# Steps of the weights' sums: every fourth tile of queries instead of every third, and two for each head of the linear attention

## The chip, the cores and the metric

The kernel runs on one core of one Trainium2 chip. The time is the device time of one execution in microseconds (us), and the profile is of one execution of the same program. PE is the engine of the matrix products, ACT the one of the activations, DVE the vector engine, POOL the GpSimd engine, SP the engine that mostly issues transfers. ACTq stands for transfers that ACT's instruction stream issues.

## The reference

One step of a layer of a hybrid decoder over 1024 new tokens of a prompt and 8 x 8 tokens of running sequences. The token mixing has two branches, softmax attention with a forget gate (8 heads) and gated linear attention (4 heads), then a GeGLU network with a convolution:

```
hn = rmsnorm(x, g_pre_mix)
q_a, k_a, v_a, logf, q_b, k_b, v_b, log_alpha, r_b, gate_a, gate_b = project_mixer_inputs(hn, ...)
o_a = attn_fn(q_a, k_a, v_a, logf)                  # forgetting attention
o_b, gla_state = gla_fn(q_b, k_b, v_b, log_alpha)   # linear attention, in chunks
o_b = rmsnorm(o_b, g_gla) * silu(r_b)
merged = sigmoid(gate_a) * (o_a @ w_proj_a) + sigmoid(gate_b) * (o_b @ w_proj_b)
x = x + rmsnorm(merged @ w_out, g_post_mix)
u = rmsnorm(x, g_pre_ffn) @ w_up                    # then convolution, gelu(g) * a, @ w_down
y = x + rmsnorm(f, g_post_ffn)
```

## The kernel before, in words

All products are made of three single products of split operands (high times high, high times low, low times high). The products with `w_up` use a scheme of Strassen's kind, which needs sums and differences of blocks of `w_up`. These sums are built early and in DRAM, by transfers alone: `ws_step` makes one step of it. Step number n issues four plain copies of quarter blocks of `w_up` into `d_ws[n]` from ACT's stream (line 195, 512 rows of 512 bytes, 256 KB each), and up to four adding transfers from POOL's stream (line 200) which belong to blocks n-1, n-2 and n-3: two that add from `w_up`, two that add one `d_ws` into another. Blocks 2 to 21 exist, so the steps run from 2 to 24, with one empty step behind them; the last steps have no copies any more. The sums are read in the network's stage, from about 1300 us on. `ws_step` gets a `pace`, an ACT instruction and a POOL instruction: its copies stand behind the first and its adding transfers behind the second.

The stages in order of time: normalisation and the first products (0 to 104 us), the forgetting attention of the prompt (104 to 459, four pairs of heads j, n = 0 to 15 tiles of queries in each), the attention of the running sequences (459 to 640), the linear attention, one head after another (640 to about 1050), merging and the output product, then the network (1300 on).

In the forgetting attention, each tile's `scores` run one tile ahead of `turn` and `values`; softmax exponentials are ACT's (line 745), 128 elements wide for a head's first tile and 128 more for each next one, eight tiles to a head. Columns of the input projection (`mm`) that are needed later are cut into units of six products and spread between the tiles by `slot()`. In the linear attention each head has a part of levels, then a part of eight chunks: for every chunk c the output `o` (line 122, three products of `ath`, `vh` and three of the running state `sth`, `qe`), copied out by ACT (`ob`, line 1251) since there is one buffer for `o`; the state's product `S`, added into `st` by DVE; and its high part `sth` made by ACT. Between them stand the decay of the next head (`e`, lines 860 to 862), the gate of the output (lines 1229 to 1231, on rows loaded from `d_r` by SP at line 1221), and units of the next head's projections with their evacuations (`q`, `k`, line 630); the groups `mm` of these units take three buffers in turn, so that a fourth group waits for the evacuation of the first. The head ends with a norm on DVE (line 1304) and turns on PE. Here `pace` is the exponential of line 1187 and the subtraction on POOL of line 1214, which stand just ahead of the first chunk. POOL then has the `km` of line 1292, needed at the end of the chunks, and the clearing of `ath` for the next head (line 1104).

The framework's scheduler sets the order of each engine's instructions from the order in which they are written and their dependences. Its hardware transfers, SP's and ACT's together, take eight completion counters in turn, so that a transfer waits until the one eight before it is done.

## Time and profile before

| | us |
|---|---|
| median of 3 runs (lowest, highest) | 2026.95 (2025.34, 2031.42) |
| the profiled execution's own time | 2028.32 |
| its span in the trace | 2026.6 |
| PE busy | 1953.4 (96%) |
| DVE, ACT, POOL busy | 1315.1, 910.8, 461.5 |

The span is the time from the first to the last recorded instruction; the execution's own time is 1.7 us longer. A row of the trace with `x2` merges equal instructions that follow each other, and its second number is then the time from the first one's start to the last one's end. What stands in brackets at a row's end is the idle time of the engine before it and what ended it.

### The profile page before, as it was taken

To read this page: it belongs to the slowest core of one execution; us is meant where nothing else is said; L and a number is where in the kernel's file an instruction comes from. 1 tells how busy PE (TensorE), PEld (TensorE's weight loads), DVE (VectorE), ACT (ScalarE), POOL (GpSimd) and SP (SyncE) were. 2 spreads that over 40 slices of the span, in tenths; PEclk is the share of its full clock that TensorE was granted. 3 is DMA by queue.
4 is the path that set the end of the run, shared out by engine and by line. 5 is a ranking of instruction groups with operands and counts; after the bars stand their busy time and mean duration, and the time that the engine had idled before them with its cause. 6 is when DMAs were issued, how large, how long until landed. Compare 5 with 4: busy or idle time off the path is not lost.

```text
span 2026.6 us, 35542 instructions
## 1 busy us (share of the span) xinstructions
PE 1953.4 (96%) x13681; PEld 1789.9 (88%) x13681; DVE 1315.1 (65%) x2635; ACT 910.8 (45%) x1734; POOL 461.5 (23%) x610
## 2 busy tenths in 40 slices
PE   6999999999999899999999999999999999999998
PEld 5899999997888788888989977899999999977886
DVE  6566665663334786868464457877677677758686
ACT  5344544442333465564544333454444444545552
POOL 2032323232110432313012221123223334210000
PEclk9999999999999999999999999999999999999999
DMA  4387979797883152423387442143444555657575
GB/s 139 96 200 182 230 184 204 172 223 269 284 267 110 43 136 60 120 60 99 105 263 233 151 156 104 41 143 129 145 132 144 195 181 171 224 194 244 175 251 158
DMA packets 302431, 335.25 MB, mean 165 GB/s; under 512 B 23327, under 2 KB 234575, under 8 KB 298165
## 3 DMA queue, kind: packets, MB, share of 16 engines
q1 hardware_dynamic: 216501, 217.37, 34.9%
q0 software_dynamic: 39488, 79.15, 15.4%
q10 hardware_dynamic: 46272, 36.44, 5.7%
q8 instruction: 108, 1.77, 0.4%
q14 instruction: 62, 0.51, 0.1%
HBM read 265.78 MB, written 113.30 MB: 187 GB/s over the span
## 4 chain that ended last, share of the span: by engine, by line
PE 77%; DVE 9%; DMA 6%; ACT 4%; issue 2%; POOL 1%; ACTq 1%; DVEq 0%; SPq 0%; POOLq 0%
PE mm L122 37%; PE dn L122 15%; PE u L122 9%; PE tp L125 5%; PE o L122 4%; PE S L122 3%; PE y L122 3%; DVE wv L128 2%; DMA d_ob<-oo 2%; DVE wlo L128 1%; DMA smk<-in_consts 1%; ACTq L195 1%; PE sm L122 1%; DMA m<-d_ob 1%; DVE act L128 1%
## 5 line engine op out<-in xcount | busy, mean ns | idle before, releaser
L122 PE MATMUL mm<-act,whi 128*128 128x384 f32 (+2 forms) x3568 | 891.1, 331 | 5.5 <-DVE act L128 3.9
L122 PEld LDWEIGHTS mm<-act,whi 128*128 128x128 f32 (+1 forms) x3568 | 617.1, 189 | 15.6 <-DVE act L128 5.4
L122 PE MATMUL mm<-act,wlo 128*128 128x384 f32 (+2 forms) x1784 | 583.2, 327 | 0.0
L122 PEld LDWEIGHTS mm<-act,wlo 128*128 128x128 f32 (+1 forms) x1784 | 336.3, 189 | 0.5
L128 DVE TENSOR_TENSOR wlo<-wraw,whi 128x1024 fp32r<-128x1024 f32 (+1 forms) x111 | 135.1, 1217 | 57.3 <-ACT whi L134 53.9
L134 ACT ACTIVATE whi<-wraw 128x1024 fp32r<-128x1024 f32 (+1 forms) x113 | 115.9, 1025 | 87.2 <-PE mm L122 79.1
L131 DVE SCALAR_TENSOR_TENSOR cv<-u,cw,cv 128x1104 f32<-128x1104 f32 x84 | 112.8, 1363 | 13.0 <-ACT cv L1556 13.0
L122 PE MATMUL dn<-dh,hhi 128*128 128x512 f32 x264 | 105.0, 400 | 2.4 <-ACT hhi L134 2.4
L122 PE MATMUL dn<-dh,hlo 128*128 128x512 f32 x264 | 104.8, 397 | 0.3 <-DVE hlo L128 0.3
L122 PE MATMUL dn<-dl,hhi 128*128 128x512 f32 x264 | 105.0, 398 | 0.0
L122 PE MATMUL y<-wo,act 128*128 128x512 f32 x416 | 99.8, 397 | 1.3 <-DVE wo L128 1.1
L122 PEld LDWEIGHTS y<-wo,act 128*128 128x128 f32 x416 | 77.1, 188 | 21.2 <-DVE wo L128 2.2
L134 ACT ACTIVATE sh<-sr 128x512 fp32r<-128x512 f32 x80 | 50.3, 633 | 87.1 <-PE u L122 33.3
L722 POOL TENSOR_SCALAR_AFFINE_SELECT bd<-cb 128x128 f32<-128x128 f32 x64 | 36.8, 582 | 179.8 <-DVE mx L739 163.3
L745 ACT ACTIVATE s<-s,ng 128x128 f32<-128x128 f32 (+3 forms) x64 | 49.6, 775 | 48.8 <-DVE ng L743 46.5
L420 ACT ACTIVATE spl<-mm 128x384 f32<-128x384 f32 (+1 forms) x72 | 33.6, 468 | 84.4 <-PE mm L122 74.4
L128 POOL TENSOR_TENSOR wv<-wv,k 128x512 f32<-128x512 f32 (+1 forms) x28 | 51.8, 1868 | 73.2 <-ACT wv L1128 72.1
L122 PE MATMUL mm<-bh,whi 128*128 128x384 f32 (+1 forms) x192 | 63.0, 328 | 3.2 <-ACT bh L134 2.6
L134 ACT ACTIVATE pth<-tp 128x512 fp32r<-128x512 f32 (+2 forms) x96 | 43.5, 488 | 49.3 <-PE tp L125 16.9
L735 DVE CUSTOM_DVE_ANT_0 s<-S,cb 128x512 f32<-128x512 f32 (+2 forms) x80 | 40.7, 527 | 37.9 <-PE S L122 32.4
L1556 ACT ACTIVATE cv<-u,cw 128x1104 f32<-128x1104 f32 x42 | 54.9, 1308 | 22.0 <-issue 10.8
L200 POOL DMA_DIRECT2D d_ws<-in_w_up x40 | 53.9, 1542 | 41.1 <-DMA d_ws<-in_w_up 40.7
(470 smaller groups left out, 4281.5 us busy)
## 6 DMA issues: line engine op xcount, KB each, us to landing
wraw<-in_w_in SPq DMA_DIRECT2D x52, 512.0 KB
wraw<-in_w_up SPq DMA_DIRECT2D x44, 512.0 KB
d_ws<-in_w_up ACTq DMA_DIRECT2D x80, 256.0 KB
sr<-d_ws SPq DMA_DIRECT2D x80, 256.0 KB
draw<-in_w_down SPq DMA_DIRECT2D x77, 256.0 KB
d_h<-cv POOLq DMA_DIRECT2D x44, 256.0 KB, 5.0
d_s<-spl POOLq DMA_DIRECT2D x44, 256.0 KB, 4.8
d_ws<-in_w_up POOLq DMA_DIRECT2D x40, 256.0 KB, 9.2
```

Of the source, the lines that this page charges most:

```text
L122: return record(pe.matmul(out, **kw))
L125: return record(pe.transpose(*args))
L128: eng.tensor_tensor(out=out, in0=a, in1=b, op=op)
L131: return dve.scalar_tensor_tensor(out=out, in0=a, scalar=s, in1=b, op0=op0, op1=op1)
L134: act.activation(out, src, AF.Copy)
L195: act.dma_start(out=d, in_=y)
L200: pool.dma_start(out=d_ws[i][d], in_=src, max_dma_last_dim=4 * P * 4, accum_op=ALU.add)
L420: act.activation(t[:, o:o + n], ps[:, :n], AF.Copy)
L722: pace[1] = pool.affine_select(out=bd, in_=cb[:, qc], pattern=[[-1, P]], compare_op=ALU.is_ge, fill=NEG, base=0, channel_multiplier=1)
L735: dve.tensor_tensor_reduce(out=s[:, k0:k0 + m], in0=ps[:, :m], in1=cb[:, k0:k0 + m], scale=1.0, scalar=-3.0e38, op0=ALU.add, op1=ALU.max, ...
L745: pace[0] = act.activation(s[:, :nk], s[:, :nk], AF.Exp, bias=ng, accum_out=sm)
L1556: act.activation(c, u[:, 2:], AF.Identity, scale=cw[:, 2, m:m + 1], bias=cw[:, 3, m:m + 1])
```

## The change

In the forgetting attention a step is made at n = 1, 5, 9, 13 of each pair of heads, and no more at n = 1, 4, 7, 10, 13: 16 steps in place of 20. In the linear attention each head makes two steps in place of one, with the same pace: 8 in place of 4. The number of all steps, 24, and their transfers stay the same.

```
@@ hybrid_step, forgetting attention
             if n < 15:
                 heads[2 * j + (n + 1) // 8][0]((qt + 1) % 8)
-                if n % 3 == 1:
+                if n % 4 == 1:
                     ws_step(*pace)
                 slot()
@@ hybrid_step, linear attention
             pace[1] = pool.tensor_tensor(out=ql, in0=qe[:, :T], in1=f(qh), op=ALU.subtract)
             ws_step(*pace)
+            ws_step(*pace)
             sil = []
```

Before, the steps of the forgetting attention were numbers 2 to 21 and held all 80 copies; the four heads of the linear attention had numbers 22 to 25, with 4, 2, 1 and 0 adding transfers. Now the forgetting attention has numbers 2 to 17, and the heads have 18 and 19, 20 and 21, 22 and 23, 24 and 25: 8, 8, 0 and 0 copies on ACT, and 8, 8, 6 and 1 adding transfers on POOL. Lines behind 1215 have a number higher by one in the changed kernel.

ACT, in the first head's chunks, before: from the copy of the first chunk's output on. `ob` is that copy, `wv` and `k` are casts of operands, `q` is the evacuation of the next head's first group of products, `e` its decay, `sth` the state's high part.

```order
L1251 ACTIVATE ob_8165<-o_8167 128x256
L1264 ACTIVATE jk_8182,gss_8166<-ob_8165 128x256
L134 ACTIVATE wv_8084<-vT_8077 128x1024
L134 ACTIVATE wv_8075<-tp_8087 128x512
L134 ACTIVATE wv_8075<-tp_8094 128x512
L630 ACTIVATE q_8157<-mm_8158 128x384
L134 ACTIVATE k_1478_7542<-tp_8101 32x128 x2
L860 ACTIVATE e_1536_8123<-tp_8121,ba_5499 128x384
L134 ACTIVATE k_1479_7543<-tp_8101 32x128 x2
L861 ACTIVATE e_1536_8123<-e_1536_8123 128x384
L134 ACTIVATE sth_8178<-st_8176 128x256
```

ACT at the same place now. Two copies (`d_ws_18_86` and `d_ws_18_87`) stand a few rows higher, ahead of the casts `wv`.

```order
L195 DMA d_ws_18_88_149<-in_w_up 512x1x128
L134 ACTIVATE k_1478_7510<-tp_8069 32x128 x2
L195 DMA d_ws_18_89_150<-in_w_up 512x1x128
L134 ACTIVATE k_1479_7511<-tp_8069 32x128 x2
L195 DMA d_ws_19_90_151<-in_w_up 512x1x128
L195 DMA d_ws_19_91_152<-in_w_up 512x1x128
L195 DMA d_ws_19_92_153<-in_w_up 512x1x128
L195 DMA d_ws_19_93_154<-in_w_up 512x1x128
L860 ACTIVATE e_1536_8103<-tp_8101,ba_5467 128x384
L1252 ACTIVATE ob_8145<-o_8147 128x256
```

All eight copies stand ahead of the first chunk's `ob`, which stood ahead of the casts before; `q` has left this place and comes 16 rows behind the last one shown, behind the gate's and the decay's exponentials.

PE, in the same chunks, before: `o_8196` is the second chunk's output, `mm` are units of the next head's projections, `tp` a turn.

```order
L122 MATMUL mm_8158<-act_107_186,wlo_8117 128x384
L122 MATMUL mm_8158<-act_107_186,whi_8116 128x384
L122 MATMUL mm_8158<-act_108_187,whi_8116 128x384
L122 MATMUL o_8196<-vh_7539,ath_7546 128x256
L122 MATMUL o_8196<-vl_7540,ath_7546 128x256
L122 MATMUL o_8196<-vh_7539,atl_7547 128x256
L122 MATMUL mm_8158<-act_107_186,wlo_8117 128x384
L122 MATMUL mm_8158<-act_107_186,whi_8116 128x384
```

PE now: the second chunk's output is `o_8176`.

```order
L122 MATMUL mm_8301<-act_111_190,whi_8096 128x320 x2
L122 MATMUL mm_8301<-act_111_190,wlo_8097 128x320
L122 MATMUL mm_8301<-act_111_190,whi_8096 128x320 x2
L122 MATMUL mm_8301<-act_111_190,wlo_8097 128x320
L122 MATMUL o_8176<-vh_7507,ath_7514 128x256
L122 MATMUL o_8176<-vl_7508,ath_7514 128x256
L122 MATMUL o_8176<-vh_7507,atl_7515 128x256
L122 MATMUL tp_8125<-al_459,wa_5466 128x320
L122 MATMUL mm_8301<-act_111_190,whi_8096 128x320
L122 MATMUL o_8176<-sth_8158,wv_8052 128x256
```

The second chunk's first products have moved 56 rows down, behind the units of two more groups; the chunks behind it follow with fewer units between them, and from the sixth chunk on the rows stand as before.

POOL, first head, before: from the subtraction of line 1214 to the clearing for the next head.

```order
L1214 TENSOR_TENSOR wv_8085<-vT_8077,wv_8084 128x1024
L200 DMA d_ws_19_93_154<-d_ws_19_91_152 128x512
L200 DMA d_ws_20_95_156<-d_ws_20_94_155 128x512
L200 DMA d_ws_21_98_159<-in_w_up 512x1x128
L200 DMA d_ws_21_100_161<-in_w_up 512x1x128
L1292 TENSOR_SCALAR km_8493<-k_1478_7542,cst_61 96x128
L1292 TENSOR_SCALAR km_8500<-k_1478_7542,cst_61 96x128
L1104 MEMSET ath_8784 128x1024
```

POOL at the same place now.

```order
L1214 TENSOR_TENSOR wv_8053<-vT_8045,wv_8052 128x1024
L200 DMA d_ws_15_77_138<-d_ws_15_75_136 128x512
L200 DMA d_ws_16_79_140<-d_ws_16_78_139 128x512
L200 DMA d_ws_17_82_143<-in_w_up 512x1x128
L200 DMA d_ws_17_84_145<-in_w_up 512x1x128
L200 DMA d_ws_18_86_147<-in_w_up 512x1x128
L200 DMA d_ws_16_81_142<-d_ws_16_79_140 128x512
L200 DMA d_ws_17_83_144<-d_ws_17_82_143 128x512
L200 DMA d_ws_18_88_149<-in_w_up 512x1x128
L1293 TENSOR_SCALAR km_8473<-k_1478_7510,cst_61 96x128
L1293 TENSOR_SCALAR km_8480<-k_1478_7510,cst_61 96x128
L1104 MEMSET ath_8764 128x1024
```

Four more adding transfers stand ahead of `km`; the fifth to the eighth of them read or add to blocks that the first four or ACT's copies of the same head write.

## Rows read from the trace of the kernel before

**Rows 1.** The page's span and its first part: busy time, share of the span and instructions of each engine.

```profile
span 2026.6 us, 35542 instructions
...
PE 1953.4 (96%) x13681; PEld 1789.9 (88%) x13681; DVE 1315.1 (65%) x2635; ACT 910.8 (45%) x1734; POOL 461.5 (23%) x610
```

**Rows 2.** Stretches of the span (us from its start): the forgetting attention, the start of the running sequences' attention, the first head's chunks of the linear attention, and the part of them in which the new copies would stand. Columns: start and end, length, busy time of each engine with its instructions, TensorE's granted clock, mean busy share of the 16 DMA engines, GB/s.

```profile
core 0: us, PE busy (x) PEld busy (x) DVE busy (x) ACT busy (x) POOL busy (x), PEclk, DMA share, GB/s
104.00:459.00 355.00, 350.05 (x2281) 338.75 (x2280) 224.17 (x671) 159.62 (x354) 102.52 (x141) 1.00 0.88 199
459.00:482.00 23.00, 19.39 (x123) 15.04 (x122) 6.62 (x12) 5.23 (x9) 5.57 (x7) 1.00 0.87 315
698.00:733.00 35.00, 34.22 (x226) 30.91 (x228) 25.38 (x54) 30.37 (x78) 11.01 (x11) 1.00 0.45 97
704.00:719.00 15.00, 14.38 (x90) 13.08 (x91) 11.20 (x24) 13.29 (x31) 7.98 (x7) 1.00 0.61 108
```

**Rows 3.** PE's waits between 100 and 451 us, and between 455 and 485 us: who waited for whom, us in total, times, the longest.

```profile
PE o L122 <- ACT pth L134: 3.6, 4, 1.0
...
PE tp L125 <- DVE kt L904: 3.5, 1, 3.5
```

**Rows 4.** The copies of line 195: least, median and longest duration in ns of one record; then three steps of the forgetting attention on ACT in order of time.

```profile
L195 ACTq DMA_DIRECT2D d_ws<-in_w_up x80: 551/647/3013, 104.5 to 444.5; - x80
...
136.61 0.40 ACT L745 ACTIVATE s<-s,ng 128x128 f32<-128x128 f32 x1 [0.54 <-DVE ng L743]
...
137.20 3.94 ACTq L195 DMA_DIRECT2D d_ws<-in_w_up  x3
141.19 1.09 ACT L134 ACTIVATE pth<-tp 128x512 fp32r<-128x512 f32 x2 [4.08 <-PE mm L122]
...
197.66 0.61 ACT L745 ACTIVATE s<-s,ng 128x384 f32<-128x384 f32 x1
...
198.77 3.70 ACTq L195 DMA_DIRECT2D d_ws<-in_w_up  x2
202.52 0.38 ACT L134 ACTIVATE pth<-tp 128x256 fp32r<-128x256 f32 x1 [4.16 <-issue]
...
208.26 1.24 ACTq L195 DMA_DIRECT2D d_ws<-in_w_up  x2
209.54 1.87 ACTq L195 DMA_DIRECT2D d_ws<-in_w_up  x2
```

**Rows 5.** PE behind four steps.

```profile
141.84 0.39 PE L122 MATMUL o<-pth,vhl 128*128 128x256 f32 x1 [0.78 <-ACT pth L134]
...
202.96 0.39 PE L122 MATMUL o<-pth,vhl 128*128 128x256 f32 x1 [0.93 <-ACT pth L134]
...
292.61 0.38 PE L122 MATMUL o<-pth,vhl 128*128 128x256 f32 x1 [0.90 <-ACT pth L134]
...
394.06 0.38 PE L122 MATMUL o<-pth,vhl 128*128 128x256 f32 x1 [0.99 <-ACT pth L134]
```

**Rows 6.** ACT in the first head's chunks, in order of time.

```profile
705.25 1.06 ACT L134 ACTIVATE wv<-vT 128x1024 fp32r<-128x1024 f32 x1 [0.24 <-DVE vT L128]
...
707.17 0.49 ACT L630 ACTIVATE q<-mm 128x384 f32<-128x384 f32 x1
...
714.25 1.11 ACT L1229 ACTIVATE wv<-vT 128x1088 f32<-128x1088 f32 x1
...
723.61 0.43 ACT L1229 ACTIVATE gs<-vT 128x272 f32<-128x272 f32 x1 [1.24 <-DMA vT<-d_r]
```

**Rows 7.** PE in the first head's chunks: the second chunk's output and the fourth chunk's.

```profile
704.52 0.39 PE L122 MATMUL o<-vh,ath 128*128 128x256 f32 x1 [0.65 <-ACT ob L1251]
...
719.38 0.28 PE L122 MATMUL o<-vh,ath 128*128 128x256 f32 x1
```

**Rows 8.** POOL in the four heads of the linear attention, in order of time.

```profile
706.46 2.40 POOL L1214 TENSOR_TENSOR wv<-vT,wv 128x1024 fp32r<-128x1024 f32 x1 [12.71 <-ACT wv L134]
708.81 1.85 POOL L200 DMA_DIRECT2D d_ws<-d_ws  x2
709.99 3.05 POOL L200 DMA_DIRECT2D d_ws<-in_w_up  x2
711.29 3.15 POOL L1292 TENSOR_SCALAR km<-k,cst 96x128 fp32r<-96x128 f32 x2
729.84 0.95 POOL L1104 MEMSET ath<- 128x1024 f32 x1 [15.41 <-PE o L122]
...
800.01 2.40 POOL L1214 TENSOR_TENSOR wv<-vT,wv 128x1024 fp32r<-128x1024 f32 x1 [12.72 <-ACT wv L134]
802.36 1.74 POOL L200 DMA_DIRECT2D d_ws<-d_ws  x2
...
892.69 2.40 POOL L1214 TENSOR_TENSOR wv<-vT,wv 128x1024 fp32r<-128x1024 f32 x1 [12.71 <-ACT wv L134]
...
986.93 2.41 POOL L1214 TENSOR_TENSOR wv<-vT,wv 128x1024 fp32r<-128x1024 f32 x1 [13.82 <-ACT wv L134]
```

**Rows 9.** SP's loads of the gate's rows in the first head (two of them, from the first's issue to the second's end), and the page's row on the queue of ACT's transfers: packets, MB, share of 16 engines' span.

```profile
708.88 11.06 SPq L1221 DMA_DIRECT2D vT<-d_r  x2
...
q10 hardware_dynamic: 46272, 36.44, 5.7%
```

3 lines of the change are left out of this document (2 added, 1 removed).

## The prediction

> **What bounds the kernel now.** I read first the page's shares of busy time. PE is busy for 1953.4 of 2026.6 us, ACT for 45%, POOL for 23% [rows 1]. So a gain has to come out of the 73 us in which PE idles, and a loss arises wherever a moved instruction makes PE wait longer. Next I read the busy time by stretches, for the two stages that the change touches. In the forgetting attention PE works 350.05 of 355 us, and in the 23 us behind it 19.39 [rows 2]. All that the change could win there is therefore 4.95 us, and 3.6 more behind it. In the first head's chunks of the linear attention PE works 34.22 of 35 us, and ACT, which has 45% over the whole span, has 30.37 of 35, and 13.29 of 15 in the first part of them [rows 2]. Eight transfers are now to be issued by ACT in just this part. Then I read PE's waits: in the forgetting attention the only one of weight is `o` for ACT's `pth`, 3.6 us in four times, and behind the stage one turn waits 3.5 us for DVE's `kt` [rows 3].
>
> **The forgetting attention: steps taken away.** One copy of line 195 holds ACT for 0.65 us in the median [rows 4]. A usual step has two rows of two, 1.24 and 1.87 us, from 208.26 to 211.41. In some steps a record is far longer: three copies take 3.94 us from 137.20, two take 3.70 us from 198.77 [rows 4]. Right behind these PE waits, 0.78 us at 141.84 and 0.93 us at 202.96 [rows 5]; that they are followed by ACT's `pth` says that the wait comes from the copies. Which tile it was is read from the exponential beside it, that runs one tile ahead: 128x128 at 136.61, the first tile of a pair's second head, so n = 7, where no step is made any more; 128x384 at 197.66, so n = 1, and that step stays [rows 4]. Two more such waits, 0.90 us at 292.61 and 0.99 at 394.06 [rows 5], are n = 1 by the same reading of the exponentials beside them. So I take off 0.8 us. The bounds: nothing, if the step that now stands at n = 5 or 9 meets the same wait in its place; 4.95 us, if PE lost all its idle time of the stage.
>
> The Trainium skill ("Perfetto Trace Analysis", section "DMA Instruction — HWDGE (DVE, Sync)") says that the record of an issue starts when its semaphores are satisfied and covers the wait for a lock, the making of descriptors and the push, and not the movement of the data. The row of 3.94 us for three copies can be read so, but no row tells what a long record waited for. By this rule a long copy would come where much is being issued or moved, whatever its place; a copy that waits only for a counter would show as a gap and not as a long record.
>
> **The first two heads of the linear attention: eight copies each.** A head had no copies here, and now eight. Their issue costs 8 x 0.65 = 5.2 us of ACT [rows 4]. The order puts them ahead of, between and behind the casts `wv` and `k`, all ahead of the first chunk's `ob` and of the decay's `e`, that is between 704 and 709 us by the times of before (the cast `wv` ran at 705.25 [rows 6]). What ACT has to set against it is its idle time: 15 − 13.29 = 1.7 us between 704 and 719 [rows 2]. The rest, 5.2 − 1.7 = 3.5 us, is delay of everything behind, on ACT first: `ob`, `e`, `sth`, the gate's exponentials from 714.25, and `q`, which before came at 707.17 [rows 6] and now stands behind them all.
>
> Does PE wait for this? The second `o` waited 0.65 us for `ob` already before, at 704.52 [rows 7]. The scheduler has answered this by writing units of two more groups of the next head's projections ahead of the second chunk's output. This covers `ob`; but with three buffers the fourth group needs the evacuation `q`, which is now later than before by the copies and by the exponentials. Those units were PE's reserve for the later chunks, and from the sixth chunk on the order is as before, so what is pulled up front is missing behind: the fourth chunk's output, at 719.38 without a wait [rows 7], follows closer on the third's, whose `ob` ACT delivers late. PE is busy for 14.38 of 15 us there [rows 2], so a wait of it can be made up nowhere and lengthens the span. I take the whole delay of ACT as PE's: 3.5 us for each head, 7.0 us for both (the second head has the same eight copies and nearly the same order).
>
> Bounds for a head. From below, nothing: if ACT's delay is used up in chunks where PE still has units. ACT idles 35 − 30.37 = 4.6 us over the longer stretch to 733 [rows 2], of which I count 3.7 us behind the copies, so that 5.2 − 3.7 = 1.5 us is a middle value. From above 8.5 us: if two of the eight copies last as the long ones of before did, (3.94 − 0.65 x 3) or (3.70 − 0.65 x 2), some 2 to 2.5 us more each [rows 4]. I stay with 3.5 us, since the row of ACT's 89% busy time is nearer to a full engine than to a free one, and the DMA share here, 0.61, is below the 0.88 of the stage in which the long copies stood [rows 2].
>
> **The same heads: the adding transfers.** POOL issues 8, 8, 6 and 1 in place of 4, 2, 1 and none, ahead of `km`. Four of before take from 708.81 to 713.04, and POOL has 15.41 us of idle time ahead of the clearing at 729.84 [rows 8]. Four more issues, and a wait for a landing between them, fit in there, and no row of PE waits for POOL in these places. The line of the subtraction starts at 706.46, 800.01, 892.69 and 986.93; the spacings are 93.55, 92.68 and 94.24 us behind 4, 2 and 1 issues [rows 8], which does not grow with the issues. I take nothing; if the cover were gone, 16 more issues at 0.43 us (the first two spacings' difference, 0.87 us, for two issues) would be 7 us.
>
> **The sum.** −0.8 + 2 x 3.5 = +6.2 us: from the profiled execution's own 2028.3 us to 2034.5 us. That execution lies 1.4 us above the median of 2026.95, so a median would come out at about 2033.
>
> **Rivals.** *First, hidden.* The units that are pulled up cover ACT's delay, and `q` comes in time. For it speaks that PE's wait ahead of the second `o` was 0.65 us only and that ACT idles 3.7 us behind; against it the 89%. From −1 us (the 0.8 us alone) to 2 x 1.5 + 0.8, about +4: 2026 to 2031 us.
>
> *Second, longer stalls.* The copies bring load on the DMA engines to a place where the gate's rows are loaded: ACT's queue moved 36.44 MB in 5.7% of the span [rows 9], 115.5 us of all 16 engines, so 0.83 us for a copy of 0.262 MB, 6.7 us for eight. In these 15 us 0.61 of them were busy, 9.2 us [rows 2]; the sum, 15.9, is more than 15. SP's load of `d_r` took until 719.94 from 708.88 with its second issue [rows 9], ACT waited 1.24 us for such a row at 723.61 [rows 6], and the first gate row is needed at 714.25, ahead of `q`. If this row comes late by the 6.7 us less some slack, or two copies take 2.5 us more, a head costs 5 to 8.5 us: +9 to +17, 2036 to 2044 us. It decides as soon as ACT waits more than about 2 us at line 1229 in either head. The Trainium skill ("DMA: Bandwidth & Descriptors", section "Issuing engines are not separate DMA queues") says that transfers issued by ACT, SP and POOL run on the same 16 engines and interleave, so that issuing them from elsewhere saves the issuer's time alone. No row of before shows copies and the gate's load side by side.
>
> *Third, faster.* The forgetting attention gives up its waits, and the stage behind it that for `kt`: sixteen copies fewer are 13 us of all DMA engines, at a share of 0.88 [rows 2, 9]. With 3.6 + 3.5 us [rows 3] and the copies hidden: about 2020 us. Against it speaks that three of the four waits follow a step that stays. It decides if less than 1 us of PE's waits is left up to 482 us.
>
> **Chances.** A measurement of this kernel can tell about 0.3%, 6.1 us, from no change. The forecast's case, +4 to +9 us, has 0.48, and half of it lies above the 6.1 us, from 2033.05 on. Hidden has 0.28, longer stalls 0.17, faster 0.07. So slower is 0.24 + 0.17 = 0.41, the same 0.24 + 0.28 = 0.52, faster 0.07. Leaving out the third rival and the upper end of the second, the range is 2025 to 2043; the forecast's own is 2031 to 2036. The predicted time is 2033.
>
> **What the changed profile would show.** If the forecast holds: copies of line 195 at about 703 to 710 and 797 to 804 us; ACT over 95% busy in the 15 us around them; PE in both heads with a wait or two of 1 to 3 us, `mm` for ACT's `q` or `o` for ACT's `ob`; and the subtraction's rows 97 and 96 us apart in place of 93.55 and 92.68, the third spacing still 94. In the forgetting attention PE's busy time within 1 us of 350 and no wait of 0.8 us near 141.8. If it is hidden, the spacings stay and ACT's idle time of before is gone. If stalls are longer, copies of over 1.5 us or a wait at line 1229 stand in the two heads. What would make it wrong above all: that ACT's lateness reaches PE in another ratio than one to one, which no row of before shows, or that the slight new order of DVE and PE in the forgetting attention moves a wait I did not look for.

## The result: the change made the kernel 1% slower, and the profile after

| | before | changed |
|---|---|---|
| median of the runs beside each other, us | 2028.9 | 2049.8 |
| ratio, 95% interval | | 1.0102, 1.0079 to 1.0125 |
| span of the profiled execution, us | 2026.6 | 2045.6 |
| PE busy, us | 1953.4 | 1966.0 |

A second set of runs gave 1.0116 (1.0095 to 1.0137). The prediction, 2033 us with a range to 2043, had the sign of its sum right (+6.2), but less than a third of the size (+20.9).

The page of the changed kernel, the same two lines as [rows 1]:

```profile
span 2045.6 us, 35539 instructions
...
PE 1966.0 (96%) x13681; PEld 1800.4 (88%) x13681; DVE 1314.7 (64%) x2635; ACT 911.0 (45%) x1734; POOL 461.6 (23%) x610
```

The number of products is the same, 13681, and PE is busy with them for 12.6 us longer. This is the first thing to see: of the 19.0 us that the span has grown, only 6.4 are more waits of PE (net of waits that went away in other stages), and the rest is products that ran slower.

POOL's subtraction ahead of the chunks of each head, in the changed kernel, answers to [rows 8]:

```profile
703.11 2.40 POOL L1214 TENSOR_TENSOR wv<-vT,wv 128x1024 fp32r<-128x1024 f32 x1 [12.71 <-ACT wv L134]
...
807.93 2.40 POOL L1214 TENSOR_TENSOR wv<-vT,wv 128x1024 fp32r<-128x1024 f32 x1 [12.71 <-ACT wv L134]
...
910.87 2.40 POOL L1214 TENSOR_TENSOR wv<-vT,wv 128x1024 fp32r<-128x1024 f32 x1 [12.71 <-ACT wv L134]
...
1006.08 2.41 POOL L1214 TENSOR_TENSOR wv<-vT,wv 128x1024 fp32r<-128x1024 f32 x1 [13.81 <-ACT wv L134]
```

The first one comes 3.35 us earlier than before (706.46): that is the forgetting attention's gain. The distance to the next is 104.82 us in place of 93.55 (+11.27), then 102.94 for 92.68 (+10.26), then 95.21 for 94.24 (+0.97). −3.35 + 11.27 + 10.26 + 0.97 = +19.15, so all of the span's 19.0 us arises up to here and nothing behind.

Now the same three stretches by busy time. First the changed kernel, from subtraction to subtraction (columns as in [rows 2]):

```profile
core 0: us, PE busy (x) PEld busy (x) DVE busy (x) ACT busy (x) POOL busy (x), PEclk, DMA share, GB/s
703.11:807.93 104.82, 95.78 (x969) 85.30 (x968) 68.79 (x151) 51.06 (x117) 31.88 (x28) 0.93 0.47 114
807.93:910.87 102.94, 94.36 (x968) 84.05 (x967) 68.66 (x151) 51.99 (x120) 30.22 (x29) 0.95 0.46 111
910.87:1006.08 95.21, 91.09 (x976) 81.45 (x976) 68.68 (x149) 52.68 (x117) 29.77 (x26) 1.00 0.41 103
```

And the kernel before:

```profile
706.46:800.01 93.55, 89.68 (x968) 80.03 (x968) 68.63 (x151) 51.36 (x117) 28.15 (x24) 1.00 0.37 94
800.01:892.69 92.68, 89.46 (x968) 80.00 (x968) 69.35 (x151) 51.37 (x117) 25.53 (x22) 1.00 0.32 90
892.69:986.93 94.24, 90.91 (x976) 81.31 (x976) 68.83 (x149) 52.71 (x117) 24.57 (x22) 1.00 0.31 90
```

In the first head PE has 968 products before and 969 now, and idles 104.82 − 95.78 = 9.04 us for 93.55 − 89.68 = 3.87: 5.17 us more. For the same products it is busy 6.10 us longer, at a mean granted clock of 0.93. In the second head it idles 5.36 us more and is busy 4.90 us longer. Half of the loss is waiting, half is the clock.

ACT in the first head's chunks of the changed kernel, which answers to [rows 6]:

```profile
699.35 1.27 ACTq L195 DMA_DIRECT2D d_ws<-in_w_up  x2
...
702.88 0.55 ACTq L195 DMA_DIRECT2D d_ws<-in_w_up  x1
...
704.88 0.55 ACTq L195 DMA_DIRECT2D d_ws<-in_w_up  x1
...
705.77 0.55 ACTq L195 DMA_DIRECT2D d_ws<-in_w_up  x1
...
706.37 3.97 ACTq L195 DMA_DIRECT2D d_ws<-in_w_up  x3
710.38 0.58 ACT L860 ACTIVATE e<-tp,ba 128x384 f32<-128x384 f32 x1 [4.07 <-issue]
710.86 0.38 ACT L1252 ACTIVATE ob<-o 128x256 f32<-128x256 f32 x1
...
718.69 0.49 ACT L630 ACTIVATE q<-mm 128x384 f32<-128x384 f32 x1
...
726.01 0.43 ACT L1230 ACTIVATE gs<-vT 128x272 f32<-128x272 f32 x1 [1.14 <-DMA vT<-d_r]
```

The eight copies take 1.27 + 3 x 0.55 + 3.97 = 6.89 us of ACT; the last three alone take 3.97, and ACT's next instruction stands 4.07 us later with no other reason than the issue. Counted from the subtraction, `ob` starts 7.75 us behind it (710.86 − 703.11) where it stood 2.38 us ahead (704.08, 706.46), and `q` 15.58 us behind it (718.69) in place of 0.71 (707.17). The gate's row is waited for about as long as before, 1.14 us at 726.01. The first `ob` in the kernel before:

```profile
704.08 0.38 ACT L1251 ACTIVATE ob<-o 128x256 f32<-128x256 f32 x1
```

PE beside it:

```profile
711.29 0.39 PE L122 MATMUL o<-vh,ath 128*128 128x256 f32 x1 [0.57 <-ACT ob L1252]
...
714.56 0.39 PE L122 MATMUL o<-vh,ath 128*128 128x256 f32 x1 [0.53 <-ACT ob L1252]
...
716.67 0.39 PE L122 MATMUL S<-vh,wv 128*128 128x256 f32 x1 [0.43 <-DVE st L131]
...
719.24 1.01 PE L122 MATMUL mm<-act,whi 128*128 128x384 f32 x2 [1.94 <-ACT q L630]
```

The waits are 0.57, 0.53, 0.43 and 1.94 us, the last one for `q`, by the fourth group of products that needs the first group's buffer. What follows is seen in stretches of 5 us of the changed kernel:

```profile
710.00:715.00 5.00, 3.89 (x24) 3.06 (x23) 3.52 (x8) 4.62 (x12) 1.67 (x2) 1.00 1.19 218
715.00:720.00 5.00, 2.45 (x10) 1.67 (x9) 4.44 (x10) 5.00 (x13) 3.38 (x4) 0.80 1.31 202
720.00:725.00 5.00, 5.00 (x21) 5.00 (x21) 2.87 (x7) 3.25 (x10) 1.47 (x2) 0.52 1.18 244
725.00:730.00 5.00, 5.00 (x34) 4.70 (x33) 2.89 (x7) 3.89 (x13) 0.00 (x0) 1.00 0.69 159
```

PE is busy for 3.89 of 5 us, then 2.45 of 5, and then the granted clock is at its lower level (0.52 is 1.2 GHz for nearly the whole stretch): 21 products where the kernel before has 34:

```profile
720.00:725.00 5.00, 4.97 (x34) 4.76 (x33) 3.50 (x9) 3.77 (x11) 0.00 (x0) 1.00 0.60 167
```

So ACT's lateness is paid twice: first as a wait, then as some 7 us at half the clock, from 718 to 725, which are worth 3.4 us. The head has a second such fall from 782 to 790, behind a wait of 2.04 us for the next head's `vT` (0.96 before). One more of the larger waits, for the norm at the head's end, is 2.20 us at 752.57 (1.33 before).

In the forgetting attention, the stretch and the wait that answer to [rows 2, 3]:

```profile
104.00:459.00 355.00, 352.60 (x2296) 341.39 (x2295) 225.13 (x672) 161.81 (x355) 88.08 (x128) 1.00 0.75 176
```

```profile
PE o L122 <- ACT pth L134: 1.4, 3, 0.7
```

PE's busy time is 352.60 for 350.05 us and the waits for `pth` are 1.4 us for 3.6; the wait at 141.84 is gone, the other three are shorter (0.57, 0.67 and 0.18 us at 201.04, 290.83 and 391.38).

### The profile page after: what moved, and what is told of

Its sections match the earlier page's. It is cut to its first block, busy times and chain, and to the rows that moved or that the text cites. A ratio compares the mean times of both kernels' runs of the same rounds, so it can differ in the third digit from the quotient of the medians.

```text
span 2045.6 us, 35539 instructions
## 1 busy us (share of the span) xinstructions
PE 1966.0 (96%) x13681; PEld 1800.4 (88%) x13681; DVE 1314.7 (64%) x2635; ACT 911.0 (45%) x1734; POOL 461.6 (23%) x610
## 4 chain that ended last, share of the span: by engine, by line
PE 75%; DVE 9%; DMA 7%; ACT 5%; issue 2%; ACTq 1%; POOL 1%; DVEq 0%; SPq 0%; POOLq 0%
PE mm L122 36%; PE dn L122 14%; PE u L122 9%; PE tp L125 5%; PE o L122 4%; PE S L122 3%; PE y L122 3%; DMA d_ob<-oo 2%; DVE wv L128 2%; ACTq L195 1%; DMA smk<-in_consts 1%; DVE wlo L128 1%; DMA m<-d_ob 1%; PE sm L122 1%; DMA out_gla_s<-so 0%
## 5 line engine op out<-in xcount | busy, mean ns | idle before, releaser
L122 PE MATMUL mm<-act,whi 128*128 128x384 f32 (+2 forms) x3568 | 901.1, 333 | 8.7 <-ACT q L630 3.9
L128 DVE TENSOR_TENSOR sl<-sr,sh 128x512 fp32r<-128x512 f32 x80 | 53.3, 684 | 17.4 <-ACT sh L134 17.4
L122 PE MATMUL mm<-bh,wlo 128*128 128x384 f32 (+1 forms) x192 | 62.6, 327 | 0.3 <-DVE wlo L128 0.3
```

Of the source, the lines that this page charges most:

```text
L122: return record(pe.matmul(out, **kw))
L128: eng.tensor_tensor(out=out, in0=a, in1=b, op=op)
```

## The experiments

Theory A was that ACT's time is the cause: the copies hold ACT, PE waits, and the clock falls behind the wait. Theory B was the bytes, wherever they are issued. Theory C was POOL's adding transfers. The first results added the order as a cause of its own, and A1 and A2 then say whether the place or the number of copies decides. All kernels are measured against the kernel before on the same chip. "Idle" in the table is PE's, in us, between two subtractions; single profiles.

| | ratio (95% interval) | first subtraction | head 1: length, idle | head 2 | head 3 |
|---|---|---|---|---|---|
| before | | 706.46 | 93.55, 3.87 | 92.68, 3.22 | 94.24, 3.33 |
| the change | 1.0102 (1.0079 to 1.0125) | 703.11 | 104.82, 9.04 | 102.94, 8.58 | 95.21, 4.12 |
| the change again | 1.0116 (1.0095 to 1.0137) | 702.98 | 104.03, 8.31 | 105.75, 11.39 | 97.16, 4.45 |
| copies alone | 1.0082 (1.0054 to 1.0110) | 715.10 | 101.17, 9.00 | 101.41, 8.57 | 94.06, 3.23 |
| no adding transfers | 1.0058 (1.0036 to 1.0081) | 706.32 | 101.67, 7.77 | 99.84, 8.03 | 94.29, 3.56 |
| two steps, no copies | 1.0014 (0.9999 to 1.0030) | 706.01 | 94.84, 5.23 | 92.62, 3.20 | 94.10, 3.14 |
| copies by SP | 1.0022 (1.0003 to 1.0041) | 704.11 | 97.10, 5.93 | 96.47, 5.36 | 95.17, 4.15 |
| quarter copies | 1.0082 (1.0058 to 1.0106) | 713.09 | 101.10, 9.10 | 99.51, 8.73 | 95.42, 4.20 |
| one step a head | 1.0087 (1.0066 to 1.0108) | 704.58 | 99.64, 7.66 | 97.27, 7.42 | 96.73, 5.85 |
| `q` behind, no copies | 1.0039 (1.0016 to 1.0063) | 706.58 | 95.23, 4.57 | 94.82, 4.33 | 95.98, 4.22 |
| gate later | 1.0024 (1.0005 to 1.0044) | 702.90 | 98.51, 7.63 | 97.99, 6.08 | 96.64, 4.64 |
| before, gate later | 1.0024 (1.0005 to 1.0042) | 705.64 | 97.36, 4.24 | 94.36, 4.27 | 95.00, 3.61 |
| wait filled | 1.0096 (1.0066 to 1.0126) | 700.94 | 104.71, 8.97 | 105.66, 8.73 | 100.51, 8.08 |
| spread over eight chunks | 1.0016 (1.0000 to 1.0031) | 705.60 | 93.98, 4.43 | 95.40, 5.12 | 99.50, 5.62 |
| spread over four heads | 1.0025 (1.0005 to 1.0046) | 705.88 | 93.52, 3.62 | 92.61, 2.48 | 93.81, 2.92 |
| behind the chunks | 1.0166 (1.0146 to 1.0187) | 705.79 | 107.09, 15.03 | 105.44, 11.08 | 100.43, 7.17 |
| in the norm | 1.0030 (1.0014 to 1.0047) | 702.30 | 93.22, 3.75 | 92.97, 3.33 | 93.80, 3.08 |
| in the merging | 1.0035 (1.0022 to 1.0047) | 703.18 | 93.30, 3.82 | 92.88, 3.27 | 93.89, 3.11 |

**The change again.**

> The changed kernel itself once more, on the chip of these runs, to compare stages: spacings 103 to 105, 102 to 104 and 95 us, ratio 1.008 to 1.012; the first subtraction between 703 and 707 us, by how many long copies the forgetting attention has this time.

The lengths of the first two heads came out as expected within 2 us, and the third head's was 2 us over. Between the two profiles of the change a head's length differs by up to 2.8 us, with the falls of the clock. Heads in which nothing was moved repeat within 0.5 us (93.22, 92.97 and 93.80 without steps, for 93.55, 92.68 and 94.24). So a difference of 2 us against the kernel before says something, and one of 2 us against the change does not.

**Copies alone.** The kernel before, its own steps untouched, with eight more copies in each of the first two heads, which nobody reads.

```
+    def more_copies(h, a):
+        with tc.issue_after(a.ins):
+            for n in range(8):
...
+                act.dma_start(out=d_no[8 * h + n], in_=wc[:, 4 * (n % 2):4 * (n % 2) + 4])
...
             ws_step(*pace)
+            if h < 2:
+                more_copies(h, pace[0])
```

> The kernel before (its steps as they were), and in the first two heads of the linear attention eight more copies of 256 KB from w_up into blocks that nobody reads, at the changed kernel's place; order of PE and ACT in the heads as in the change. It has neither the change's gain in the forgetting attention nor its eight adding transfers a head. If copies and the order they bring are the whole loss: spacings 101 to 105 us in the first two heads, 94.2 in the third, ratio 1.009 to 1.013. If the adding transfers or the other steps matter: 96 us or less.

```profile
715.10:816.27 101.17, 92.17 (x969) 81.83 (x968) 68.40 (x151) 51.04 (x117) 26.28 (x25) 0.98 0.42 108
816.27:917.68 101.41, 92.84 (x968) 82.29 (x967) 68.37 (x151) 51.96 (x120) 23.78 (x23) 0.97 0.35 98
```

```profile
731.47 0.89 PE L122 MATMUL mm<-act,whi 128*128 128x384 f32 x2 [1.94 <-ACT q L638]
```

The first block is the two heads, the second the unit that waits for `q`: 1.94 us, to the hundredth the wait of the change. Idle time, 9.00 and 8.57 us, is that of the change too. The copies and the order they bring suffice for the waiting, and give 7.6 and 8.7 of the 11 us a head. (The first subtraction at 715.10 is late by waits in the forgetting attention, 8.3 us for `pth` in place of 3.6, though its steps are those of before; this profile is the slowest of the kernel's four runs, so I leave that stage out.)

**Two steps, no copies**: the change's second line alone.

```
-                if n % 4 == 1:
+                if n % 3 == 1:
                     ws_step(*pace)
```

> The second part of the change alone: steps at n % 3 == 1 as before, two steps a head; no copy is left for the linear attention, and its seven adding transfers stand in the first two heads. Orders of PE, ACT and DVE are those of before. Theory A and B: the kernel before within 1 us, spacings 93.5, 92.7 and 94.2. Theory C: 1 to 3 us for the first head, which has six adding transfers for four.

Nothing in the second and third head; 1.3 us in the first, which has six adding transfers for four. With no copy beside it, ACT waits there for the second gate's row, 1.24 us before [rows 6] and 3.18 here, and PE waits 1.95 us for the `ob` behind it:

```profile
725.06 0.43 ACT L1230 ACTIVATE gs<-vT 128x272 f32<-128x272 f32 x1 [3.18 <-DMA vT<-d_r]
```

Issuing two steps there is nearly free as long as they hold no copy; but two more adding transfers are enough to make this row late.

**No adding transfers** in the linear attention (this leaves the sums of the last blocks out).

```
-                if i in d_ws:
+                if i in d_ws and adds:
...
-            ws_step(*pace)
-            ws_step(*pace)
+            ws_step(*pace, False)
+            ws_step(*pace, False)
```

> The changed kernel without the adding transfers of the linear attention (the sums of the last blocks are left out); the order of all engines is otherwise that of the changed kernel. Theory A: spacings of 102 to 105 us as with the change. If the adds' traffic is what makes the eighth copy long: 96 to 99 us, time 2032 to 2038. Theory C: 93 us, time 2023 to 2028.

The heads are 3 us shorter than with the change, the last three copies take 2.02 us in place of 3.97, and PE still waits 1.9 us for `q`. In neither of the two heads does ACT wait for the second gate's row: in the first, ACT takes it 4.4 us behind the issue of its load (721.1 to 725.52), where the change has it after 6.0 us (720.0 to 726.01). Theory C falls as the main cause. The adds have a part of some 3 us a head, more of it in busy time (93.90 and 91.81 for 95.78 and 94.36 us) than in idle time, that is, in how long the clock is low. (3 us is hardly more than the change's own spread; what carries it is the ratio, 1.0058 for 1.0116, on the same chip, whose intervals do not meet.)

**Copies by SP.**

```
-                    act.dma_start(out=d, in_=y)
+                    eng.dma_start(out=d, in_=y)
...
-            ws_step(*pace)
-            ws_step(*pace)
+            ws_step(*pace, sp)
+            ws_step(*pace, sp)
```

> The changed kernel, but the sixteen copies of the first two heads of the linear attention are issued by SP in place of ACT; bytes, place and pace stay. Theory A (ACT's time: eight issues, the last one long, hold ACT; PE waits and its clock falls behind the wait): with ACT free the loss is gone, the subtraction's rows are 93.5 and 92.7 us apart as before (104.8 and 102.9 with the change), the first of them stays near 703 us (706.5 before), and the time is 2023 to 2028 us. Theory B (the bytes on the DMA engines, wherever they are issued, make loads late): the spacings stay above 100 us and the time above 2040. Theory C (the eight adding transfers of POOL): the spacings stay as with the change, 103 to 105 us.

Neither theory had this: 7 us of the 11 go, 4 stay. With ACT free the order is that of before, and `q` is not waited for. What stays is in this row of ACT:

```profile
724.00 0.43 ACT L1231 ACTIVATE gs<-vT 128x272 f32<-128x272 f32 x1 [3.73 <-DMA vT<-d_r]
```

The second gate's row is waited for 3.73 us, 1.24 before [rows 6], and PE waits 2.61 us for the `ob` behind it. This is the wait of the prediction's second rival. SP issues the row's load no later than before (717.2, 13.1 us behind the subtraction; 719.6 and 13.1 before), so it is the load that takes longer: ACT has the row 6.8 us behind the issue, for 4.0 before. In the change itself the wait is covered in part, since ACT comes late to this row anyway (1.14 us; but 2.64 us in the second head of the change run again). The Trainium skill ("DMA: Bandwidth & Descriptors", section "Issuing engines are not separate DMA queues") says that moving the issue saves the issuer's time alone, since all transfers share the 16 engines; the run agrees in that 4 us a head are left. But it does not show that these are the copies': the eight adding transfers run beside the row's load too.

**Quarter copies.** All copies whole in the forgetting attention, five to a step (`late` adds the fifth), and the eight of each head once more with 128 of their 512 rows.

```
-                for d, y in zip(d_ws[n], (x21, x11, x11, x12)):
+                own = list(zip(d_ws[n], (x21, x11, x11, x12)))
+                own = own if n < 18 else [(d[:, :1], y[:, :1]) for d, y in own]
+                for d, y in own + list(late(n)):
                     act.dma_start(out=d, in_=y)
```

> All 80 copies are made whole in the forgetting attention (five in each of its 16 steps), and in the first two heads of the linear attention ACT issues the same eight copies a head once more, each with a quarter of its rows (128 of 512 B), which writes the same values again. The order of the engines in these heads is that of the changed kernel. Theory A with the long eighth copy due to the issue as such: it stays near 2.4 us, spacings 103 to 105 us. Theory A with the long eighth copy due to what is still in the queue: eight copies of 0.6 us, some 2 to 3 us less of delay on ACT, PE's wait for q under 1 us and no fall of the clock there, spacings 95 to 98 us, time 2030 to 2036. Theory B: no loss at all, 93 us, time below 2028. Theory C: 103 to 105 us.

No long record is left, the longest is 0.615 us, so a long copy comes of what is in flight and not of the issue. But the heads are still 101.10 and 99.51 us: my expectation of 95 to 98 fails. The eight issues take 4.5 us still, the order is that of the change, and `q` is waited for 1.82 us; then the second gate's row comes late:

```profile
733.67 0.43 ACT L1240 ACTIVATE gs<-vT 128x272 f32<-128x272 f32 x1 [3.72 <-DMA vT<-d_r]
```

So the waiting, half of the loss, needs no long copy. And the late row needs no bytes of the copies: it is waited for 3.72 us with a quarter of them, as with all of them by SP (3.73), and 3.18 us with none and six adding transfers; with whole copies and no adding transfers ACT does not wait for it at all. This points, for the change, to the fifth to eighth adding transfer, which POOL issues from 714 on, beside the row's load at 720. (The first subtraction at 713.09 comes of waits for `pth` in the forgetting attention, 7.7 us. That five copies a step are the cause is not shown: the copies alone had 8.3 us there with four.)

**One step a head**, four copies in each of four heads, in the change's order.

```
             ws_step(*pace)
-            ws_step(*pace)
+            if h == 3:
+                for _ in range(4):
+                    ws_step(*pace)
```

> Steps at n % 4 == 1, then one step in each of the four heads at the changed kernel's place (four copies each, as many as 4 in heads 2 and 3 too), and the last four steps, which have adding transfers alone, behind the last head's. The order of ACT and PE in the first chunks is that of the changed kernel: q behind the gate's exponentials. If the loss goes by the number of copies held in ACT (0.65 us each and the long eighth): spacings of 95 to 96 us in three heads and no fall of the clock, ratio 1.001 to 1.003. If the new order itself makes PE wait: mm waits 1.5 to 2 us for q and the clock falls behind it in each head, spacings 98 to 101 us in all three, ratio 1.006 to 1.012, as much as the change with half the copies a head.

```profile
PE mm L122 <- ACT q L630: 3.7, 3, 1.2
```

Half the copies give 6.1 and 4.6 us of loss, 54% and 45% of the change's, and 2.5 us in the third head, where the change has no copies; PE waits up to 1.2 us for `q` in each. The last subtraction is 11.3 us late, and some 7 us more are lost behind it, where the last head holds the last copies and steps. The ratio is that of the second expectation, and so is the first length; the other two lie between the two expectations. Only the first head has a fall of the clock that shows in PE's busy time (91.98 us for 89.68).

**`q` behind, no copies.** The kernel before, with the evacuation `q` tied behind the first gate's exponentials.

```
+            if behind and o == 0:
+                with tc.issue_after(behind[0].ins):
+                    act.activation(dst[:, o:o + n], ps[:, :n], AF.Copy, scale=scale)
+                return
...
-        return ev_copy(t[name], DKB ** -0.5 if name == "q" else 1.0)
+        return ev_copy(t[name], DKB ** -0.5 if name == "q" else 1.0, gate_end if name == "q" and h else None)
```

> The kernel before, with one tie more: in each head of the linear attention the evacuation q of the next head's first group stands on ACT behind the first gate's exponentials, as it came to stand in the changed kernel; no copies in these heads. If the order makes the loss by itself: mm waits 1 to 2 us for q, spacings of 97 to 101 us, ratio 1.005 to 1.009. If it needs the held copies too: ACT reaches q early enough, no wait of mm for q over 0.5 us, spacings 93 to 95.5 us, ratio 0.999 to 1.003.

```profile
719.09 0.62 PE L122 MATMUL mm<-act,whi 128*128 128x384 f32 x2 [0.30 <-ACT q L632]
```

The wait for `q` is 0.30 us, and the heads lose 1.7, 2.1 and 1.7 us. The order alone is cheap, some 2 us a head; it needs the copies to become dear.

**Gate later, with the change and without.** Both gates are written one chunk later, so that `q` stands ahead of the exponentials again. The copies stay where the change has them.

```
-                if h < 3 and c in (1, 3):
-                    gate(c // 2)
+                if h < 3 and c in (2, 4):
+                    gate(int(c == 4))
```

> The changed kernel with the two gates of a head written behind its third and fifth chunk in place of the second and fourth, so that ACT has q ahead of the first gate's exponentials again; copies, their place and their number are those of the change. If q's place in ACT's order makes the longest wait: no wait of mm for q, spacings of 98 to 101 us, ratio 1.004 to 1.008. If the held copies alone make the loss: the wait moves on to o for ob, spacings stay at 103 to 105, ratio 1.010 or more.

> The kernel before with the same move of the gates, as control of the last run: if the move is worth nothing by itself, spacings 93.5, 92.7 and 94.2 within 1.5 us, ratio 0.998 to 1.002.

```profile
702.90:801.41 98.51, 90.88 (x969) 80.98 (x968) 69.52 (x151) 50.63 (x117) 30.31 (x28) 0.98 0.50 122
801.41:899.40 97.99, 91.91 (x968) 82.78 (x967) 67.83 (x151) 51.64 (x120) 30.33 (x29) 0.97 0.49 117
```

No unit waits for `q`, and the heads (first and second) are 98.51 and 97.99 us. The control was not free, though: 97.36 and 94.36 us, and 1.0024. On this base the change costs nothing that can be measured, 1.0024 against 1.0024 (in the profiles 1.2, 3.6 and 1.6 us more in the heads, 2.7 us less up to the first subtraction). The same two steps at the same place cost 11 us a head with one order of ACT's instructions, and 1 to 4 with another (5 against the kernel before, whose first head is 3.8 us shorter than the control's).

**Wait filled.** The change, with 16 products that nobody reads put ahead of the unit that waits for `q`.

```
                 three(pst[:, :DVB], [(kth[:, c, :], ktl[:, c, :], vh[:, c, :], vl[:, c, :])])
+                if h < 2 and c == 4:
+                    for _ in range(16):
+                        mm(pst[:, DVB:], lhsT=kth[:, c, :], rhs=vh[:, c, :], start=True, stop=True)
```

> The changed kernel with 16 products of 128x256 put in each of the first two heads right ahead of the unit that waits 1.94 us for ACT's q; they write columns that nobody reads, and all orders are otherwise those of the changed kernel. Sixteen at about 0.107 us are 1.7 us, so they fill the wait and should lengthen nothing by themselves. If the clock falls there because PE stood idle: it stays at 1.00 between 715 and 725 us, the wait for q is 0.2 us, and each of the two heads gets some 3 us shorter than the change's 103 to 105 us, ratio about 1.006 to 1.009. If the clock falls for another reason (the transfers beside it): it falls as before, spacings 103 to 106 us, ratio 1.010 to 1.012.

```profile
715.00:720.00 5.00, 4.98 (x36) 4.60 (x35) 4.66 (x10) 4.88 (x14) 4.14 (x4) 1.00 1.26 205
720.00:725.00 5.00, 3.44 (x23) 2.96 (x21) 2.10 (x4) 1.73 (x5) 0.00 (x0) 1.00 1.19 277
725.00:730.00 5.00, 3.66 (x16) 3.66 (x17) 2.11 (x5) 4.12 (x15) 0.00 (x0) 0.66 0.13 37
```

```profile
724.67 0.43 ACT L1230 ACTIVATE gs<-vT 128x272 f32<-128x272 f32 x1 [3.27 <-DMA vT<-d_r]
```

```profile
726.34 0.58 PE L122 MATMUL o<-vh,ath 128*128 128x256 f32 x1 [2.91 <-ACT ob L1252]
```

The clock stays at 1.00 from 715 to 725 us: it follows PE's idling and not the transfers beside it, whose share is as high as in the change (1.26 and 1.19). But the heads got no shorter, against what I expected, even counting 1.7 us that the idle products take. ACT, no longer behind, now waits 3.27 us for the second gate's row, PE 2.91 us for the `ob` behind that, and the clock falls there, from 725 on (0.66). Closing one gap opens the next. In the change, two causes stand nearly level: ACT's lateness, which the copies make, and a load that is late beside the adding transfers.

**The place.** Four kernels move the last steps elsewhere. *Spread over eight chunks*: one copy behind the square of each chunk's output (the second part of the cut stands in the loop over chunks), adding transfers one head later.

```
-            ws_step(*pace)
-            ws_step(*pace)
+            for n in ((18,), (19, 20), (21, 22), (23, 24))[h]:
+                ws_adds(n, pace[1])
...
+                if h < 2:
+                    ws_copies(18 + 2 * h + c // 4, sq, [c % 4])
```

> The changed kernel with the eight copies of a head one by one behind the square of each chunk's output, and the adding transfers that need them one head later, at the old place. Eight issues of 0.6 us in the chunks, none back to back. Theory A1: each one delays one chunk's ACT work by 0.6 us, in chunks in which ACT idles 4.6 us of 35; 0 to 3 us a head, spacings 93 to 97 us, ratio 0.999 to 1.003. Theory A2: 97 us and more, ratio 1.004 or more.

Eight copies on ACT cost 0.4 us in the first head and 2.7 in the second; theory A1 holds there, since the same number back to back costs 7.6 and 8.7 without any more adding transfers. The third head, with eight adding transfers that were put off and no copies, loses 5.3 us: ACT waits 3.31 us for the second gate's row, PE 2.2 us for the `ob` behind it. In the first head, whose adding transfers are the four of before, this row is waited for 2.69 us beside the copies issued at 717.7 and 720.7; so it is late by whatever runs beside its load, and copies that stand there do it too.

*Spread over four heads*: the same, with four copies a head, behind every second chunk.

```
+            for n in ((18,), (19,), (20,), (21,))[h]:
+                ws_adds(n, pace[1])
...
+                if c % 2:
+                    ws_copies(18 + h, sq, [c // 2])
...
+            if h == 3:
+                for n in (22, 23, 24):
+                    ws_adds(n, pace[1])
```

> Steps at n % 4 == 1, then one step a head in all four heads with its four copies one by one behind the square of every second chunk, and its adding transfers at the old place; the last three steps behind the last head's chunks. Order of the chunks as before (q ahead of the gate). If spread copies are hidden and the forgetting attention keeps some 2 us: spacings 93 to 95.5 us, ratio 0.997 to 1.000. If each copy still delays its chunk: 95 to 97 us, ratio 1.001 to 1.004.

The three heads are as before or shorter, as in the first expectation, and yet the whole is 0.25% slower. The loss has moved to the last head, here from 985 us on, and then the kernel before:

```profile
985.00:1100.00 115.00, 104.50 (x616) 95.69 (x616) 60.15 (x140) 54.38 (x114) 30.14 (x31) 0.96 0.88 256
```

```profile
986.00:1101.00 115.00, 108.90 (x674) 100.95 (x673) 63.71 (x145) 57.64 (x117) 20.20 (x23) 1.00 0.74 239
```

PE is busy 4.4 us less in the same 115 us, at a granted clock of 0.96 for 1.00 and a DMA share of 0.88 for 0.74.

*Behind the chunks*: both steps behind the head's last square and last `km`.

```
-            ws_step(*pace)
-            ws_step(*pace)
...
+            for _ in range(2):
+                ws_step(sq, last_km)
 
             rs = rsqrt_mean(gp, ss, P, DVB, cols=10)
```

> The changed kernel, with both steps of a head moved behind the head's last square of outputs (ACT) and last masked key (POOL); the eight copies stay on ACT and stay as large, and the order of PE and ACT in the chunks is that of before. Theory A1 (the place decides: the copies stand where PE soon needs ACT's ob and q): the subtraction's rows are 93 to 95 us apart in all heads, no wait of mm for q, clock full in the chunks, ratio to the kernel before 0.998 to 1.001. Theory A2 (eight issues of ACT or their bytes cost wherever they stand in a head): spacings of at least 97 us, ratio 1.004 or more.

ACT was busy for 14.50 us in the 47 from 745 to 792 before, and I expected no cost. It is the worst of all. In the first head, PE, SP and ACT:

```profile
763.29 0.69 PE L125 MATMUL tp<-idt,ob 128*128 128x128 f32 x2 [12.22 <-DVE oo L128]
```

```profile
745.78 8.13 SPq L1277 DMA_DIRECT2D sb<-in_state_gla  x2
```

```profile
742.29 14.53 ACTq L195 DMA_DIRECT2D d_ws<-in_w_up  x7
```

Seven copies are spread over 14.53 us, pauses between them included. SP's two loads of the state span 8.13, the stores `d_ob` behind them start only at 757.14, and as there are two buffers `oo`, PE waits 12.22 us. What SP waited for between 735 and 770 us:

```profile
SPq L1277 <- DMA wraw<-in_w_in: 7.4, 1, 7.4
...
SPq L1323 <- DMA d_ws<-in_w_up: 3.4, 2, 3.2
```

The second load of the state waits 7.4 us for the landing of a load of `wraw` whose data it does not need. Between the two, SP and ACT issued five copies, two stores and the first load, so `wraw` is some eight transfers before it: this is how SP would be held by the completion counters, which the transfers of both take in turn. The stores then wait 3.2 us for a copy of which they need nothing either. Neither wait stands in the kernel before. Why `wraw` and the copies took so long to land is not isolated; I put it down to the bytes in flight.

*In the norm* and *in the merging* (first and second part of the cut, from one kernel each): no step in the linear attention, so its three heads are as before and the forgetting attention's part stands alone.

```
+            if i < NT - 1:
+                ws_step(*pace)
...
+                if g == 1:
+                    ws_step(a, b)
```

> Steps at n % 4 == 1 as in the change, none in the linear attention, and the last eight steps behind the squares and products with g_post_mix in the norm of the mixing's output (about 1200 to 1290 us). The order of the linear attention is that of before, so this is the forgetting attention's part of the change alone. Spacings 93.5, 92.7 and 94.2; the first subtraction 0.8 to 3.5 us earlier than before. If the eight steps are hidden there: ratio 0.998 to 1.000. If their copies hold up the loads and stores of the norm as those behind the heads did: 1.003 or more.

> Steps at n % 4 == 1 as in the change, none in the linear attention, and one step in each of the eight columns of the branches' merging (about 1090 to 1190 us), behind the second group's cast on ACT and sum on POOL. DMA share there was 0.48 in the kernel before. If the four copies of a step hide where they stand alone, 12 us apart: spacings 93.5, 92.7 and 94.2, the merging as long as before, ratio 0.997 to 0.999, the forgetting attention's 2 us and more kept. If they hold up the loads of w_proj_b and the spilled gates: the merging 3 us longer or more, ratio 1.000 to 1.004.

```profile
PE tp L125 <- DVE act L128: 12.0, 2, 10.5
```

```profile
PE mm L122 <- ACT whi L134: 4.7, 1, 4.7
PE mm L125 <- DVE sg L128: 2.7, 1, 2.7
```

The last head's subtraction comes at 982.29 and 983.25 us (986.93 before): 3.7 to 4.6 us gained. Both lose more than this where the steps went: the norm waits 12.0 us for `act` (first block; 1.9 before), the merging 4.7 and 2.7 us for weights and gates (second block). I found no version that beats the kernel before.

## Why the prediction was wrong

**The forgetting attention: sign right, too small.** Forecast −0.8, found −3.35, inside the bounds. That "three of the four waits follow a step that stays" was read rightly: they stand at 201.04, 290.83 and 391.38. But they were taken to keep their length, and this failed: 0.57, 0.67 and 0.18 us for 0.93, 0.90 and 0.99. I put this down to long copies coming of what is in flight, since there is less (DMA share 0.75 for 0.88). So 2.2 of the 3.35 us are waits for `pth`; The wait for `kt` behind the stage is 1.4 us shorter too (2.1 us for 3.5), but not clearly by the change, as a kernel with the old steps has 2.2 there (`q` behind, no copies). Over the runs, the first subtraction came between 700.9 and 706.3 us in the twelve profiles with four copies at n % 4, and between 705.6 and 706.6 in four of the five with n % 3 (the fifth at 715.1): some 2 us.

**The held copies: right in kind, a third too small.** 8 x 0.65 = 5.2 us were 6.89 and 7.71, because the last three copies took 3.97 and 4.80; long copies stood in my bound from above and not in my value. Less the 1.7 us of idle time they give 5.2 and 6.0 us of delay, and PE's idle time grew by 5.17 and 5.36. So "the whole delay of ACT as PE's" held for the waiting. By luck in part: 0.9 us of the 5.17 are the wait for the norm at the head's end, which the new order gives without any copy (2.1 us in `q` behind, no copies), and the filled wait and copies by SP show that a second cause, the gate's row, gives PE waits of 2.6 to 2.9 us when ACT is less late.

**The missing term: the clock.** The sum has none, and it is what made the forecast wrong. I priced a wait of PE at its own length, although the trace of before has a stretch with waits and a lower clock (640 to 700 us: PE busy 53.04 of 60, granted clock 0.94). Found: 6.10 and 4.90 us a head. With it, and with what was found for the other terms, the sum is −3.35 + 2 x 5.3 + 11.0 + 1 = +19.

**The adding transfers: "nothing" was wrong** by about 3 us a head, if the difference between the change and the run without them is taken. Idle time of POOL covers their issue, but what runs beside them is slower: the last three copies take 3.97 us with them and 2.02 without, and the second gate's row reaches ACT 6.0 us behind its issue with them and 4.4 without. How this lengthens the time at the lower clock is not settled.

**`q` and the three buffers: right.** The wait is where the prediction put it, with 1.94 us in both heads, and the third head's spacing stayed near 94 (95.21, and 97.16 in the second profile). The copies stand at 699 to 710, for 703 to 710 foreseen.

**The rivals.** "Hidden" had the units pulled up cover ACT's delay; they do not. "Longer stalls" named both things that happened, a long eighth copy and a late gate's row, at 0.17, and was decided by the row at line 1229 in the first place; that row shows no longer wait in the change's first profile (1.14 and 1.11 us), because ACT reaches it late, and 2.64 us in one head of the second. It laid the late row to the copies' bytes, and the runs lay it to the adding transfers. Its price, +9 to +17, would have been nearest.

**What stays open.** The falls of the clock differ between profiles of one kernel (PE's busy time in the change's third head is 91.09 us at a clock of 1.00 in one, 92.71 at 0.98 in the other). I can say that a fall comes behind idling and what it costs; not which idling brings one.

## What to carry to other kernels

Where PE runs without a pause, price a wait twice: its length, and the stretch at the lower clock behind it, which was as much again in the change (6.10 and 4.90 us for 5.17 and 5.36) and a quarter to a half of the wait with quarter copies (2.32 and 1.32 us for 5.23 and 5.51). Work that is moved off a busy stage should be read as a burst at its new place: eight copies cost 0.4 and 2.7 us spread one by one, some 8 us a head in a row ahead of evacuations that PE needs, and 12 us in one wait where an idle ACT issued them among SP's loads and stores, with which its transfers share completion counters. Count the transfers that go along with it as well: the adding ones were thought free and made a load late that PE waits for in the end. After a move, look in the new order for an evacuation that has slipped behind long independent work; with the slip undone, the same steps at the same place cost 5 us a head in place of 11.

## What the runs showed that I had not expected

The clock fell behind waits of 0.57, 0.53, 0.43 and 1.94 us within 8 us, none of them long: PE was busy for 6.3 of 10 us, and then ran some 7 us at 1.2 GHz (21 products in 5 us for 34). When 16 idle products filled the longest wait, the clock stayed full at a DMA share of 1.2 to 1.3. And one issue on ACT took up to 2.4 us in the first head and 3.0 us in the second, at the end of a row of eight; with a quarter of the rows none took over 0.62 us. Last, SP waited 7.4 us for the landing of a transfer that it needed nothing from, which stood some eight transfers back.
